# Steady pairs of the fast matrix product: P2 beside P7 instead of P5, and T4 made by VectorE from P2's tile

## The chip, the cores and the metric

The kernel runs on one core of a Trainium2 chip. The core has a matrix engine (TensorE), three engines for elementwise work (VectorE, ScalarE, GpSimd), an engine that mostly issues transfers (SyncE), and 16 DMA engines between the chip's memory and the on-chip buffers. The metric is the device time of one execution in microseconds (us), the median of several runs. In views of the profile PE is TensorE's matmuls, PEld its weight loads, DVE VectorE, ACT ScalarE, POOL GpSimd and SP SyncE.

## The reference, cut to what matters

Two layers of a mixer with 512 tokens of width 2048 in f32. Each layer normalises, multiplies by a wide input matrix w_in, runs an attention, a short convolution and a cross-attention on parts of the result, gates them and multiplies by an output matrix w_o.

```python
for l in range(DEPTH):
    h = rmsnorm(x, pre_norm_g[l])
    z = h @ w_in[l]
    q_lat, kv_lat, k_pe, gb, gc, xin, q_mem, gate = split_cols(z)
    ...
    y = jnp.concatenate([a_out, c_out, m_out], axis=-1) * jax.nn.silu(gate)
    o = y @ w_o[l]
    x = x + rmsnorm(o, post_norm_g[l])
```

The change touches only how part of `h @ w_in[l]` is computed.

## The kernel before

**The product.** `z = h @ w_in` is done in column groups. A group takes two column blocks of w_in, 512 wide each (416 in the group of the latents), and multiplies them by h with seven half-size products instead of eight (the scheme of Strassen and Winograd). h is cut into four quarters A11, A12, A21, A22 by tokens and by depth, the group's weights into B11, B12 (upper half of the depth, first and second column block), B21, B22 (lower half). The left operands (A11, A12, A22 and four sums S1 to S4) are made once a layer (`combine`, L394) and kept. The right operands are, with the signs as the code has them: P1 uses B11, P2 uses B21, P5 uses T1 = B11 + B12, P6 uses T2 = T1 + B22, P4 uses T4 = T2 + B21, P3 uses B22, P7 uses B22 + B12. T1, T2 and T4 grow in place, in the tile "T" that was loaded as B11.

**Blocks.** Each product runs over its depth in four blocks, c = 0 to 3. One block is a unit of weights (128 partitions x 1024 values, or 832) and 12 matmuls: two token tiles, two depth tiles, three matmuls each (`mm3`, L250). Three, because every f32 operand is split in a high part in the engine's f32r format and a low part, and high by high, high by low and low by high are added up. So the second matmul of a block needs the low part of the weights, the first only the high part. A product's result stays in PSUM until c = 3; `ended` (L463) then evacuates it with ScalarE or VectorE into the output tiles.

**Preparing a unit.** `prep` (L158) issues, for each unit, a cast on ScalarE (L177, tile "wh") and a subtraction on VectorE (L178, tile "wl") of the raw weights "wr". The pools of high and low parts have three buffers each; so the cast of a block waits until TensorE is done with the block three before it. Sums listed in a unit's `sums` are added before the split (L168), those in `then` after it (L186). If a later product uses the same tile with more added, `more` (L152) issues an accumulating DMA from GpSimd's queue (L137) right after the split.

**Loading.** `load` (L140) issues a unit's DMA on SyncE's queue (also L137), in the order of the units, up to eight units beyond the step at hand. Raw tiles "wr" live in a pool of eight buffers (`RAW, PIECES, SLABS = 8, 4, 19`); a load waits, on SyncE, until a buffer is free, which is when the last operation on the tile that held it has ended. The loads behind it in SyncE's queue wait too.

**Order.** TensorE, SyncE and GpSimd run in the program's order throughout. ScalarE and VectorE do so only in the opening stage; after it their order is a planner's, made when the program is built. A layer has five groups of w_in: two with the order HEAD, then three with the order STEADY: "gm, qm" (gate part and memory queries), "lat" (the latents, 416 columns) and "ga" (gate parts). The output projection uses SECOND and LATE. In an order such as `[["P1"], ["P5", "P2"], ...]` an inner list is a pass over c, in which the named products take turns. In the last steady group of a layer two small steps of four transposes each (`turn4`, L764) follow every second block, from the group's 17th block to its 28th and last.

**Buffers in a steady group.** T holds four raw buffers from P1 to P4. P2's four tiles are loaded into the other four, and each is freed after its split; B22's four tiles follow into these (P3, and after accumulating B12, P7). The next group's T comes into the buffers that P7's splits free, its P2 tiles into those that P4's splits free.

**Lazy work.** Elementwise work that is not urgent is put on a list; each step has a `room` (L551) that says how much of it may be issued beside it.

Of the kernel before, what the change touches and what calls it, by code (L numbers as in the profile page):

```python
# [207 lines left out]
def encoder(tc, x, mem, positions, pre_norm_g, w_in, q_norm_g, w_uq, kv_norm_g, w_ukv, conv_w,  # L208
# [200 lines left out]
        split("S3", a21)  # L409

    HEAD = [["P1"], ["P2"], ["P5"], ["P6", "P3"], ["P7"], ["P4"]]
    STEADY = [["P1"], ["P5", "P2"], ["P6", "P3"], ["P7"], ["P4"]]
    SECOND = [["P2"], ["P1"], ["P5"], ["P6", "P3"], ["P7"], ["P4"]]
    LATE = [["P2"], ["P1"], ["P5", "P6", "P3"], ["P7"], ["P4"]]

    def group(left, key, w, block, slot, passes, final, hold=None, by_two=False, direct=None):
# [24 lines left out]
        def unit(q, c):  # L441
            def of(name, loads=(), more=None, sums=(), then=(), **kw):
                at = {"B11": (0, 0), "B12": (0, 1), "B21": (1, 0), "B22": (1, 1)}
                k = lambda n: (key, n, c)
                return Unit(k(name), {k(to): [block(*at[n], c)] for to, n in loads}, more and block(*at[more], c),
                            [(k(a), k(b)) for a, b in sums], [(k(a), k(b)) for a, b in then], **kw)
            if q == "P1":
                return of("P1" if apart else "T", [("P1" if apart else "T", "B11")])
            if q == "P2":
                return of("P2", [("P2", "B21")])  # L450
            if q == "P4":
                return of("T", more="B21", alloc=hold)
            if late:
                return {"P5": lambda: of("T", [("B12", "B12")], sums=[("T", "B12")], place=place),
                        "P6": lambda: of("T", [("B22", "B22")], sums=[("T", "B22")]),
                        "P3": lambda: of("B22", then=[("B12", "B22")]),
                        "P7": lambda: of("B12")}[q]()
            return {"P5": lambda: of("T", [("T", "B11")] if apart else [], more="B12"), "P6": lambda: of("T", more="B22"),
                    "P3": lambda: of("B22", [("B22", "B22")]), "P7": lambda: of("B22", more="B12")}[q]()
# [3 lines left out]
        def ended(q, tt):  # L463
            ps = bk[q][tt][:, :w]
            s = {(i, j): slot(i, j, tt) for i in range(2) for j in range(2)}
            if q == "P1":
                if apart:
                    nc.scalar.copy(s[1, 0], ps)
                elif passes is STEADY:
                    nc.scalar.copy(s[0, 0], ps)  # L470
# [79 lines left out]

        def room(q, c):  # L551
            if c < 3:
                return 0.2 if late and q in ("P5", "P6", "P3") else 1.4
            moves = {"P1": shared, "P2": not shared, "P5": apart, "P7": 1 + apart, "P4": apart or direct is not None}
            return (0.2 if late and q in ("P5", "P6", "P3") else 1.4) - 1.4 * moves.get(q, 1)

        out = []
        for k, names in enumerate(passes):
            if names == ["P4"] and hold:
                out.append([(whole("P4"), [unit("P4", c) for c in range(4)], 4.0)])  # L560
                continue
            steps = [(step(q, c), [unit(q, c)], room(q, c)) for c in range(4) for q in names]
            if names == ["P7"] and hold:
                steps[1:] = [s + (4,) for s in steps[1:]]
            if by_two and k == 0:
                steps[:2] = [(two(names[0], 0), [unit(names[0], c) for c in range(2)], 0.0, 1)]
            out.append(steps)
# [58 lines left out]
    def projection(l):  # L626
        def block(cols, w):
            def f(h, j, c):
                r = h * 1024 + c * 256
                return w_in[l, r:r + 256, cols[j]:cols[j] + w].rearrange("(a p) c -> p a c", p=P)  # L630
            return f
# [9 lines left out]
        def slot_of(a, b):  # L641
            return lambda i, j, tt: C[(a, b)[j]][:, 2 * i + tt, :]
# [17 lines left out]
        def own_lat():  # L660
# [8 lines left out]
            group(L, (l, 1), 512, block((O_GB, O_G + 1024), 512), slot_of("gb", "gg"), HEAD, fin_g),  # L669
            group(L, (l, 2), 512, block((O_G + 1536, O_QM), 512), slot_of("gm", "qm"), STEADY, skip),  # L670
            group(L, (l, 3), 416, block((0, 416), 416), lat, STEADY, skip),
            group(L, (l, 4), 512, block((O_G, O_G + 512), 512), slot_of("ga0", "ga1"), STEADY, skip),
        ]
# [102 lines left out]
    def gate_turn(j, view, c):  # L776
        def f():
            ps = turn4(view, c)
            nc.scalar.activation(y_slab(j // 4)[:, j % 4, :], ps, AF.Silu)
        return f  # L780
# [13 lines left out]
    def qm_turn(j, C):  # L794
        def f():
            if j == 0:
                G["Qm"] = tuple(slab(n, F32R).rearrange("p (i c) -> p i c", i=4) for n in ("QmH", "QmL"))
            ps = turn4(lambda t: C["qm"][:, t, :], j)
            hi, lo = G["Qm"][0][:, j, :], G["Qm"][1][:, j, :]
            nc.scalar.activation(hi, ps, AF.Copy, scale=SC_MEM)  # L800
            nc.vector.scalar_tensor_tensor(lo, ps, SC_MEM, hi.bitcast(F32), op0=ALU.mult, op1=ALU.subtract)
        return f
# [480 lines left out]
    for l in range(depth):  # L1283
# [83 lines left out]
        more = [(f, []) for f in lat + [qm_turn(j, C) for j in range(4)] + [gate_turn(12 + j, gm, j) for j in range(4)]]  # L1367
# [76 lines left out]
```

## Time and profile before

| | us |
|---|---|
| median of 3 runs (lowest, highest) | 1505.4 (1505.35, 1508.21) |
| the profiled execution | 1509.11 |
| its span, first to last instruction | 1507.3 |
| granted TensorE clock, mean | 0.998 |
| transfers | 267.19 MB, mean 177 GB/s |
| accumulating and other transfers of GpSimd's queue | 45.0% of 16 engines' span |
| transfers of SyncE's queue | 27.9% |

How to read it: the page is one execution on the chip. Busy time is the time in which an engine has an instruction of its own; matmul ends are modelled, so for TensorE the distance between the starts of matmuls says more than busy time. In a row of the groups by line stand line, engine, operation, output<-inputs, form and count, then busy us and mean ns, then the engine's idle time ahead of these instructions and who ended it. In the timeline a row is start, duration, engine, line, operation; what stands in square brackets is the idle time ahead and who ended it. The steady groups begin at about 174.5, 254.3 and 318.8 us in layer 0 and at 965.0, 1044.9 and 1108.0 us in layer 1.

### The profile page before, as it was taken

How to read it: one execution, taken by the hardware profiler on the slowest of the kernel's cores; microseconds unless marked ns; L12 is line 12 of the kernel's file. 1: busy time of each engine (PE TensorE's matmuls, PEld its weight loads, DVE VectorE, ACT ScalarE, POOL GpSimd, SP SyncE). 2: the span in 40 equal slices, each digit the busy share in tenths (PEclk: the TensorE clock that was granted, in tenths of full speed). 3: DMA queues.
4: the chain of work that ended last, by engine and by line, in shares of the span. 5: the costliest groups of instructions: out<-in, count | busy, mean ns of one | idle time of the engine just before them, and what ended most of it. 6: DMA issues, size and time to landing. Idle time of an engine off the chain costs nothing.

```text
span 1507.3 us, 20232 instructions
## 1 busy us (share of the span) xinstructions
PE 1487.8 (99%) x7613; PEld 1279.3 (85%) x7613; DVE 1055.9 (70%) x1420; ACT 871.5 (58%) x1359; POOL 285.0 (19%) x277
## 2 busy tenths in 40 slices
PE   9999999999999999999999999999999999999997
PEld 7788888988898888888898888788988888988886
DVE  6965675555877668769788765575565586698687
ACT  7743534454757868645688533534464587686443
POOL 1233131332000000130310233131333000003211
PEclk9999999999999999999999999999999999999999
DMA  9999897989582112595987999898999521028945
GB/s 331 217 214 224 200 177 168 190 209 250 164 259 84 62 30 69 99 213 163 314 300 233 236 222 214 203 174 168 198 211 211 157 71 43 29 84 140 253 123 182
DMA packets 142581, 267.19 MB, mean 177 GB/s; under 512 B 17084, under 2 KB 39956, under 8 KB 139156
## 3 DMA queue, kind: packets, MB, share of 16 engines
q0 software_dynamic: 59072, 128.99, 45.0%
q1 hardware_dynamic: 83280, 136.88, 27.9%
q8 instruction: 59, 0.97, 0.3%
q14 instruction: 38, 0.31, 0.1%
q10 hardware_dynamic: 132, 0.05, 0.0%
HBM read 251.20 MB, written 14.68 MB: 176 GB/s over the span
## 4 chain that ended last, share of the span: by engine, by line
PE 83%; issue 5%; ACT 3%; DMA 3%; POOL 3%; DVE 2%; POOLq 0%; DVEq 0%; ACTq 0%
PE P L253 19%; PE P L254 19%; PE P L252 19%; POOL wr L137 3%; PE ptp L1017 2%; DMA wr<-in_w_in_dram 2%; PE tps L768 2%; DMA wr<-in_w_o_dram 1%; PE o L253 1%; PE o L254 1%; PE o L252 1%; PE sc L252 1%; PE sc L253 1%; PE sc L254 1%; PE mk L253 1%
## 5 line engine op out<-in xcount | busy, mean ns | idle before, releaser
L178 DVE TENSOR_TENSOR wl<-wr,wh 128x1024 fp32r<-128x1024 f32 (+1 forms) x400 | 476.0, 1194 | 312.7 <-ACT wh L177 304.2
L177 ACT CAST wh<-wr 128x1024 fp32r<-128x1024 f32 (+1 forms) x400 | 411.4, 1032 | 456.6 <-PE P L254 372.4
L253 PE MATMUL P<-wl,S 128*128 128x512 f32 (+1 forms) x896 | 344.1, 384 | 2.2 <-DVE wl L178 2.0
L252 PE MATMUL P<-wh,S 128*128 128x512 f32 (+1 forms) x896 | 345.4, 386 | 0.3 <-ACT wh L177 0.3
L254 PE MATMUL P<-wh,S 128*128 128x512 f32 (+1 forms) x896 | 343.4, 383 | 0.0
L137 POOL DMA_DIRECT2D wr<-in_w_in_dram x160 | 193.5, 1209 | 483.3 <-DVE wl L178 353.6
L252 PE MATMUL P<-wh,A 128*128 128x512 f32 (+1 forms) x656 | 253.1, 386 | 0.1
L253 PE MATMUL P<-wl,A 128*128 128x512 f32 (+1 forms) x656 | 252.0, 384 | 0.8 <-DVE wl L178 0.8
L254 PE MATMUL P<-wh,A 128*128 128x512 f32 (+1 forms) x656 | 251.8, 384 | 0.5 <-DVE A L258 0.5
L253 PEld LDWEIGHTS P<-wl,S 128*128 128x128 f32 x896 | 168.2, 188 | 33.2 <-DVE wl L178 3.6
L252 PEld LDWEIGHTS P<-wh,S 128*128 128x128 f32 x896 | 168.1, 188 | 30.7 <-ACT wh L177 1.1
L254 PEld LDWEIGHTS P<-wh,S 128*128 128x128 f32 x896 | 168.2, 188 | 30.3
L137 POOL DMA_DIRECT2D wr<-in_w_o_dram x40 | 48.4, 1210 | 530.7 <-DVE wl L178 516.3
L254 PEld LDWEIGHTS P<-wh,A 128*128 128x128 f32 x656 | 123.1, 188 | 23.3 <-DVE A L258 1.2
L253 PEld LDWEIGHTS P<-wl,A 128*128 128x128 f32 x656 | 123.2, 188 | 23.0 <-DVE wl L178 1.6
L252 PEld LDWEIGHTS P<-wh,A 128*128 128x128 f32 x656 | 123.1, 188 | 22.2 <-ACT wh L177 0.6
L1003 ACT ACTIVATE P<-sc,nm 128x512 f32<-128x512 f32 (+1 forms) x96 | 59.7, 622 | 31.2 <-DVE nm L1000 31.2
L1006 ACT ACTIVATE P<-P,rec 128x512 f32<-128x512 f32 (+1 forms) x96 | 63.1, 660 | 6.6 <-DVE rec L1005 6.6
L1000 DVE TENSOR_REDUCE nm<-sc 128x1 f32<-128x512 f32 (+1 forms) x96 | 57.0, 593 | 9.7 <-PE sc L998 6.2
L258 DVE TENSOR_TENSOR PT<-ptp,PT 128x512 fp32r<-128x512 f32 (+1 forms) x96 | 54.8, 593 | 10.0 <-ACT PT L257 9.6
L183 DVE SCALAR_TENSOR_TENSOR wl<-wr,cols,wh 128x512 fp32r<-128x512 f32 x64 | 45.8, 746 | 13.5 <-ACT wh L182 13.5
L182 ACT ACTIVATE wh<-wr,cols 128x512 fp32r<-128x512 f32 x64 | 43.8, 723 | 19.0 <-PE mk L253 7.8
(281 smaller groups left out, 2208.4 us busy)
## 6 DMA issues: line engine op xcount, KB each, us to landing
wr<-in_w_in_dram POOLq DMA_DIRECT2D x128, 512.0 KB, 7.3
wr<-in_w_in_dram SPq DMA_DIRECT2D x112, 512.0 KB, 5.9
wr<-in_w_o_dram SPq DMA_DIRECT2D x48, 512.0 KB, 4.2
wr<-in_w_o_dram POOLq DMA_DIRECT2D x40, 512.0 KB, 7.3
wr<-in_w_in_dram POOLq DMA_DIRECT2D x32, 416.0 KB, 5.7
wr<-in_w_in_dram SPq DMA_DIRECT2D x24, 416.0 KB, 4.1
wr<-in_w_mk_dram SPq DMA_DIRECT2D x16, 512.0 KB, 6.1
wr<-in_w_mv_dram SPq DMA_DIRECT2D x16, 512.0 KB, 5.4
```

What stands on the lines that cost most here:

```text
L137: engine.dma_start(dst, src, **kw)
L177: nc.scalar.copy(hi[:, :n], src)
L178: nc.vector.tensor_tensor(lo[:, :n], src, hi[:, :n].bitcast(F32), op=ALU.subtract)
L182: nc.scalar.activation(hi[:, h], src[:, h], AF.Copy, scale=g)
L183: nc.vector.scalar_tensor_tensor(lo[:, h], src[:, h], g, hi[:, h].bitcast(F32), op0=ALU.mult, op1=ALU.subtract)
L252: nc.tensor.matmul(ps, ah, bh, start=first, stop=False, **kw)
L253: nc.tensor.matmul(ps, ah, bl, start=False, stop=False, **kw)
L254: nc.tensor.matmul(ps, al, bh, start=False, stop=last, **kw)
L258: nc.vector.tensor_tensor(lo, src, hi.bitcast(F32), op=ALU.subtract)
L1000: nc.vector.tensor_reduce(nmax, ps, axis=AX.X, op=ALU.max, negate=True)
L1003: nc.scalar.activation(pt, ps, AF.Exp, bias=nmax, accum_out=tot)
L1006: nc.scalar.activation(pt, pt, AF.Copy, scale=rec)
```

## The change

In the order STEADY, P2 leaves the pass of P5 and takes turns with P7. After the split of P2's unit c, VectorE adds P2's tile (B21) into T (which holds T2 by then), and the accumulating DMA that added B21 to T for P4 goes away. P2's steps leave less room for lazy work. HEAD, SECOND and LATE stay as they are.

```diff
-    STEADY = [["P1"], ["P5", "P2"], ["P6", "P3"], ["P7"], ["P4"]]
+    STEADY = [["P1"], ["P5"], ["P6", "P3"], ["P7", "P2"], ["P4"]]
...
             if q == "P2":
-                return of("P2", [("P2", "B21")])
+                return of("P2", [("P2", "B21")], then=[("T", "P2")] if passes is STEADY else ())
             if q == "P4":
-                return of("T", more="B21", alloc=hold)
+                return of("T", more=None if passes is STEADY else "B21", alloc=hold)
...
         def room(q, c):
             if c < 3:
+                if passes is STEADY and q == "P2":
+                    return 0.4
                 return 0.2 if late and q in ("P5", "P6", "P3") else 1.4
```

## The prediction

> **What bounds the kernel now.** I read the page's busy times first, then TensorE's waits, then the stretches of the three steady groups in each layer, then the order of events inside one group.
>
> ```profile
> PE 1487.8 (99%) x7613; PEld 1279.3 (85%) x7613; DVE 1055.9 (70%) x1420; ACT 871.5 (58%) x1359; POOL 285.0 (19%) x277
> ```
> ```profile
> 254.30:318.80 64.50, 63.64 (x337) 62.49 (x336) 32.70 (x37) 31.96 (x49) 18.72 (x16) 1.00 0.95 202
> ...
> sum 450.50, PE 449.64 PEld 393.42 DVE 271.87 ACT 214.79 POOL 124.29; mean PE 74.94 PEld 65.57 DVE 45.31 ACT 35.80 POOL 20.71
> ```
>
> The first column pair is the stretch and its length, then busy time by engine, granted clock, DMA share, GB/s. TensorE is the bound: over the six steady groups (450.50 us) it sits idle 0.86 us, all of it in the latents group of layer 0, where the DMA engines are 95% busy. So the change can only win back what stands in this place:
>
> ```profile
> 305.92 0.34 PE L254 MATMUL P<-wh,S 128*128 128x416 f32 x1
> 306.52 0.46 PE L252 MATMUL P<-wh,S 128*128 128x416 f32 x1 [0.26 <-ACT wh L177]
> 307.58 0.46 PE L253 MATMUL P<-wl,S 128*128 128x416 f32 x1 [0.60 <-DVE wl L178]
> 307.88 0.35 PE L254 MATMUL P<-wh,S 128*128 128x416 f32 x1
> 308.07 0.35 PE L252 MATMUL P<-wh,S 128*128 128x416 f32 x1
> ```
> ```profile
> 295.98 9.51 DMA wr<-in_w_in_dram
> 305.48 0.02 issue
> 305.50 0.04 ACTq L177
> 305.54 0.04 issue
> 305.58 0.90 ACT wh L177
> ```
> ```profile
> 305.58 2.46 ACT L177 CAST wh<-wr 128x832 fp32r<-128x832 f32 x3 [5.15 <-DMA wr<-in_w_in_dram]
> ```
>
> Matmuls of 416 columns start 0.19 us apart. Here the starts are 0.60, 1.06 and 0.30 apart, so the stall costs 0.41 + 0.87 + 0.11 = 1.4 us. It is P7 with c = 3: its accumulating DMA took 9.51 us to land, between the accumulates of P4. The last row shows what a late transfer does on ACT: after 5.15 us of idleness it ran three casts back to back, so the two behind the waiting one had stood in its queue. ACT starts 0.1 us after the landing (295.98 + 9.51 = 305.49, cast at 305.58).
>
> What decides the forecast is another resource, the eight raw buffers. In a steady group four hold T from P1 to P4 and the other four hold P2's tiles, then B22's. SyncE's loads wait for them:
>
> ```profile
> SPq L137 <- DVE wl L178: 28.7, 8, 12.9
> ```
> ```profile
> 228.36 1.22 DVE L178 TENSOR_TENSOR wl<-wr,wh 128x1024 fp32r<-128x1024 f32 x1 [1.49 <-ACT wh L177]
> ```
> ```profile
> 229.61 0.37 SPq L137 DMA_DIRECT2D wr<-in_w_in_dram  x1
> ```
> ```profile
> 229.61 4.70 DMA wr<-in_w_in_dram
> ```
> ```profile
> 232.51 0.39 PE L252 MATMUL P<-wh,S 128*128 128x512 f32 x1
> ...
> 235.23 0.39 PE L252 MATMUL P<-wh,S 128*128 128x512 f32 x1
> 235.46 0.39 PE L253 MATMUL P<-wl,S 128*128 128x512 f32 x1
> ```
>
> The first row is SyncE's own waits from 229 to 250 us (total, times, longest): all eight loads of that stretch, from P7 to the end of P4, were held back by a subtraction that had not yet freed its buffer. The next rows follow the first of them, from VectorE, SyncE, the chain of waits and TensorE in turn. The subtraction of P7's first block ends at 229.58, SyncE issues 0.03 us later, and that load lands after 4.70 us. P7's first block starts on TensorE at 232.51, the next at 235.23: a block takes 2.72 us, and its second matmul (0.23 us in) is the first that needs the low part. Before, that load was for the next group, many blocks ahead, so its wait cost nothing.
>
> **The change, part by part.** Prices of single operations:
>
> ```profile
> L178 DVE TENSOR_TENSOR wl<-wr,wh 128x1024 fp32r<-128x1024 f32 x344 | 418.8, 1222 | 252.3 <-ACT wh L177 243.8 <-PE ptp L1017 7.5
> L177 ACT CAST wh<-wr 128x1024 fp32r<-128x1024 f32 x344 | 361.8, 1055 | 393.2 <-PE P L254 316.0 <-DVE wr L168 27.5 <-DMA wr<-in_w_in_dram 17.7
> L137 POOL DMA_DIRECT2D wr<-in_w_in_dram x160 | 193.5, 1209 | 483.3 <-DVE wl L178 353.6 <-DMA wr<-in_w_in_dram 87.1 <-issue 19.3
> L178 DVE TENSOR_TENSOR wl<-wr,wh 128x832 fp32r<-128x832 f32 x56 | 57.2, 1025 | 60.5 <-ACT wh L177 60.4
> L177 ACT CAST wh<-wr 128x832 fp32r<-128x832 f32 x56 | 49.6, 889 | 63.5 <-PE P L254 56.4 <-DMA wr<-in_w_in_dram 7.1
> L168 DVE TENSOR_TENSOR wr<-wr,wr 128x1024 f32<-128x1024 f32 x8 | 9.8, 1221 | 0.1
> ```
>
> *Removed:* 24 of the 160 accumulates (4 x 3 groups x 2 layers), 24 x 1.21 = 29.0 us of GpSimd and 16 x 0.52 + 8 x 0.43 = 11.8 MB. GpSimd bounds nothing. The worth on the path is at most the 1.4 us stall; I take it whole, since P7's accumulates now come every second block with no P4 accumulates among them. Bounds: nothing, if another transfer is late there, and 1.4. **-1.4.**
>
> *Added:* 24 additions on VectorE, 16 x 1.22 + 8 x 1.02 = 27.7 us. VectorE is busy 271.87 of 450.50 us here, so the time fits. Queued behind each addition is the subtraction of P7's next block: it ends 2.44 us after P2's, and is wanted 2.72 us after. That margin of 0.28 covers it; without it the price is at most some 1 us a group, 6 in all, kept for the upper end. I take 0.
>
> *Moved with no price taken:* P2's two evacuations a group go beside P7's, both off the path. P6's accumulate now follows P5's preparation by four blocks instead of eight, 10.9 us less 2.7 for cast, subtraction and issue, against this landing time:
>
> ```profile
> wr<-in_w_in_dram POOLq DMA_DIRECT2D x128, 512.0 KB, 7.3
> ```
>
> The 0.9 us that remain cover it; a landing of 9.51 would cost 1.3 a group. SyncE's queue: P2's loads move behind B22's, and the next group's T and (layer 0, last group) mem's loads behind P2's, all wanted eight or more blocks later.
>
> *Moved, and on the path: P2's loads.* When P7's first block is prepared, T and B22 fill all eight buffers. P2's first tile can only be loaded after that subtraction, one block before TensorE wants it.
>
> First load, 512 columns, on the clock of the rows above (load at 229.61): landed 234.31, cast from 234.40 to 235.46, subtraction to 236.71, wanted 235.46: late by **1.3 us**.
>
> Second load: it takes whichever buffer is freed first, by the T4 addition at 236.71 + 1.22 = 237.93 or, if the casts keep program order, by P7's second subtraction after it. A quiet load:
>
> ```profile
> wr<-in_w_mv_dram SPq DMA_DIRECT2D x4, 512.0 KB, 3.8
> ```
> ```profile
> wr<-in_w_in_dram SPq DMA_DIRECT2D x7, 416.0 KB, 3.5
> ```
>
> Issued 237.96, landed 241.76, cast and subtraction 2.4: 244.16. Wanted two blocks after the first, 236.71 + 5.44 = 242.15: late by **2.0**. Each pair frees two buffers and uses one, so the third and fourth loads are issued about two blocks earlier than needed: 0.
>
> The 416-column group:
>
> ```profile
> 295.95 1.03 DVE L178 TENSOR_TENSOR wl<-wr,wh 128x832 fp32r<-128x832 f32 x1 [1.23 <-ACT wh L177]
> ```
> ```profile
> 299.34 0.35 PE L252 MATMUL P<-wh,S 128*128 128x416 f32 x1
> ...
> 301.59 0.35 PE L252 MATMUL P<-wh,S 128*128 128x416 f32 x1
> 301.78 0.35 PE L253 MATMUL P<-wl,S 128*128 128x416 f32 x1
> ```
>
> Load at 297.00 (after 296.98), landing +4.70 = 301.70, cast to 302.68, subtraction to 303.73, wanted 301.78: **1.95**. Second: 1.02 + 0.03 + 3.5 + 0.09 + 0.89 + 0.03 + 1.02 = 6.58, less two blocks of 2.25: **2.1**. In the last steady group two turns of four transposes follow each pair, 8 x 0.109 = 0.87 us of other TensorE work:
>
> ```profile
> 1189.27 3.93 PE tps L768 x36
> ```
>
> So there 1.3 and 2.0 - 0.87 = 1.1.
>
> *The waits this adds.* On ACT the cast of P2's tile waits for the landing; behind it in the queue is the cast of P7's next block, whose data is long there and whose subtraction would free the next buffer: hence the second load's lateness. On VectorE P2's subtraction waits for the cast, the T4 addition and P7's next subtraction for it. On SyncE P2's load waits for the buffer, and behind it stand the next three and the next group's T. TensorE waits for P2's low part, and since it is the bound each of its waits is added to the end; it works off the blocks behind at 2.72 us each and makes nothing up.
>
> The unknown is the landing time: 4.70 is the row with the same neighbours (an accumulate issued just ahead), 3.3 the quickest, 9.51 the slowest. I take 4.70 for the first, the quiet medians for the second.
>
> ```profile
> wr<-in_w_in_dram SPq DMA_DIRECT2D x1, 416.0 KB, 3.3
> ```
>
> The Trainium skill, DMA: Bandwidth & Descriptors, section "Anatomy of one DMA", gives a DMA as 2.0 us and its bytes over 436 GB/s; my estimate from it is 3.2 us for 512 KB and 3.0 for 416, and the sum would then be +5.2. The trace has 3.8 and 3.5 when quiet, 4.70 beside an accumulate, so the rows decide.
>
> **Sum.** A layer: (1.3 + 2.0) + (1.95 + 2.1) + (1.3 + 1.1) = 9.75; two layers 19.5; less 1.4: **+18.1 us**. The profiled execution is 1507.3 of span and 1.8 around it, 1509.1, so it would be 1527.2. The median shown is 1505.4, 3.7 below it; I forecast on the median: 1523.5, own range 1517 to 1530.
>
> **The rivals.**
>
> *Casts out of program order.* ACT's order is the planner's there. Does it put P7's second cast before P2's first, that buffer is freed before 236 and the second load is in time. Then the first loads alone remain: 2 x (1.3 + 1.95 + 1.3) = 9.1, less 1.4: +7.7, 1513. For it: ACT would have idled. Against: the three casts in a row at 305.58.
>
> *Quick loads.* Each lands in 3.3 us, as in the row above. First loads 0, 0.55, 0; second 1.4, 1.9, 0.5: 4.35 a layer, 8.7 - 1.4 = +7.3, 1513. This is the side on which the Trainium skill's formula for a DMA lies. Against: the accumulate for P7's last block is in flight at the first load.
>
> *No slower.* Both together at the first and second P2 block: only 2 x 0.55 remains against the 1.4 won, -0.3, 1505. It decides where the load after P7's first subtraction lands within 3.4 us and P7's second cast goes ahead. More than 1.4 us cannot come from these groups, so faster by over 3 us has no mechanism I can find.
>
> *Late in every pair.* If the second buffer of a pair isn't freed before the next load wants it, three loads a group pay the second price: (1.3 + 6.0) + (1.95 + 6.3) + (1.3 + 3.3) = 20.15 a layer, +38.9, 1544. Against: two buffers are freed a pair.
>
> **How the numbers follow.** Forecast 0.50, order 0.20, quick loads 0.10, no slower 0.12, late in every pair 0.05, faster 0.03. A measurement tells some 0.2%, 3 us, from no change. Slower: 0.50 + 0.20 + 0.10 + 0.05 = 0.85; same 0.12; faster 0.03. The range takes in the forecast's own and both cases at 1513, and ends in the middle of the "no slower" case: 1506 to 1532.
>
> **What would show it.** In each steady group TensorE waits on ACT's cast and then VectorE's subtraction at P2's first and second block, 1 to 2 us each, released by a DMA of SyncE, whose issue follows the first subtraction of P7 by 0.03 us. The waits of SyncE name that subtraction and L186's addition. The wait at 306 is gone. Wrong if P2's tiles are loaded before P7 begins, or if P2's blocks show no wait on TensorE.

## The result, and the profile after

The changed kernel takes 1524.5 us in the median of 4 runs (1523.3 to 1526.5), the kernel before 1506.1 (1505.4 to 1508.2). The ratio is 1.0119, 95% interval 1.0107 to 1.0132: slower by 18 us. The profiled execution of the changed kernel is the fastest of its four, 1523.3 us with a span of 1521.4, while that of before, 1509.1 us with a span of 1507.3, was slower than its four; so the two traces lie only 14.1 us apart. The forecast was 1523.5.

The page after, and TensorE's waits (what waited, for whom; total us, times, longest):

```profile
PE 1492.3 (98%) x7613; PEld 1280.2 (84%) x7613; DVE 1082.1 (71%) x1444; ACT 870.5 (57%) x1359; POOL 256.1 (17%) x253
```
```profile
PE P L253 <- DVE wl L178: 6.9, 11, 0.8
PE P L252 <- ACT wh L177: 6.1, 7, 2.6
```

VectorE has 24 instructions and 26 us more, GpSimd 24 fewer and 29 us less, as reckoned. TensorE has the same 7613 matmuls. What grew is its waits for a cast (0.3 us before) and for a subtraction (2.8 before), in the three steady groups of each layer. The worst of the six stretches, before and after, and the six together after (length, busy time by engine, clock, DMA share, GB/s):

```profile
1044.90:1108.00 63.10, 63.10 (x338) 62.58 (x337) 33.74 (x46) 32.22 (x49) 19.03 (x16) 1.00 0.98 207
```
```profile
1052.20:1120.70 68.50, 65.33 (x337) 63.96 (x337) 38.37 (x53) 31.87 (x49) 14.31 (x12) 0.98 0.75 166
...
sum 466.20, PE 454.54 PEld 393.62 DVE 297.84 ACT 213.08 POOL 95.35; mean PE 75.76 PEld 65.60 DVE 49.64 ACT 35.51 POOL 15.89
```

TensorE sits idle 11.7 us here instead of 0.9, and the DMA engines are less busy than before (0.75 in the latents group of layer 1, 0.98 before). So the kernel waits in a stage with fewer transfers, not more: it waits for the start of one. The chain of waits in the first steady group (start, length, what):

```profile
217.25 1.24 DVE wl L178
218.49 0.02 issue
218.50 5.24 DMA wr<-in_w_in_dram
223.74 0.02 issue
223.76 1.22 DVE wr L186
224.99 1.17 DVE wl L178
226.15 0.02 issue
226.17 3.97 DMA wr<-in_w_in_dram
230.14 0.02 issue
230.16 1.23 DVE wr L186
231.39 1.18 DVE wl L178
232.57 0.04 issue
232.61 0.50 PE P L253
```

This is the forecast chain but for one step, the second load. P7's first subtraction ends at 218.48, and the load of P2's first tile is issued at 218.50; the subtraction of that tile ends at 226.15, and the load of the second tile goes at 226.17, where the forecast had it wait for the addition behind that subtraction. All six second loads leave 0.02 us after the subtraction of P2's first tile. TensorE between them, and ACT's casts:

```profile
223.90 0.39 PE L254 MATMUL P<-wh,S 128*128 128x512 f32 x1
224.94 0.49 PE L252 MATMUL P<-wh,A 128*128 128x512 f32 x1 [0.65 <-ACT wh L177]
226.20 0.50 PE L253 MATMUL P<-wl,A 128*128 128x512 f32 x1 [0.76 <-DVE wl L178]
```
```profile
223.84 1.99 ACT L177 CAST wh<-wr 128x1024 fp32r<-128x1024 f32 x2 [6.62 <-DMA wr<-in_w_in_dram]
230.24 2.95 ACT L177 CAST wh<-wr 128x1024 fp32r<-128x1024 f32 x3 [4.40 <-DMA wr<-in_w_in_dram]
```

The tile names show the place: P7 reads S, P2 reads A. The first P2 matmul starts 1.04 us after its predecessor and the second 1.26 us after that, where 0.227 is the pace. ACT sat idle for 6.62 us and then ran P2's cast and, right behind it, the one of P7's next block.

The time lost at P2's blocks, summed from the starts of TensorE's matmuls as far as they are over 0.227 us apart (0.189 in the latents groups), in us; the forecast's pairs are the first and the second block:

| group (layer, name) | first P2 block | second | forecast |
|---|---|---|---|
| 0, gm and qm | 1.95 | 0.95 | 1.3, 2.0 |
| 0, latents | 2.33 | 0.81 | 1.95, 2.1 |
| 0, ga | 1.98 | 0 | 1.3, 1.1 |
| 1, gm and qm | 1.86 | 0.51 | 1.3, 2.0 |
| 1, latents | 4.48, and 0.63 at the next block | 0 | 1.95, 2.1 |
| 1, ga | 1.60 | 0 | 1.3, 1.1 |
| sum | 14.2 + 0.6 | 2.3 | 9.1, 10.4 |

Together 17.1 us, against 19.5 forecast; the third and fourth P2 blocks lose nothing. Less the 1.4 us of P7 in the latents group of layer 0, which are gone, and 2.0 at three other last blocks of P7 outside the steady groups, which are shorter in this trace (0.96, 1.38 and 0.40 us became 0.69, 0 and 0), that is 13.7 of the 14.1 us between the spans.

### The profile page after: what moved, and what is told of

Same layout as the page of the kernel before. It is cut to its first block, busy times and chain, and to the rows that moved or that the text cites. A ratio compares the mean times of both kernels' runs of the same rounds, so it can differ in the third digit from the quotient of the medians.

```text
span 1521.4 us, 20175 instructions
## 1 busy us (share of the span) xinstructions
PE 1492.3 (98%) x7613; PEld 1280.2 (84%) x7613; DVE 1082.1 (71%) x1444; ACT 870.5 (57%) x1359; POOL 256.1 (17%) x253
## 4 chain that ended last, share of the span: by engine, by line
PE 88%; DMA 3%; DVE 3%; ACT 3%; issue 1%; POOL 1%; POOLq 0%; DVEq 0%; ACTq 0%
PE P L253 20%; PE P L254 20%; PE P L252 20%; DMA wr<-in_w_in_dram 3%; PE ptp L1019 2%; PE tps L770 2%; DVE wl L178 1%; PE o L253 1%; PE o L254 1%; PE o L252 1%; PE sc L252 1%; PE sc L253 1%; PE sc L254 1%; PE mk L253 1%; PE mk L254 1%
## 5 line engine op out<-in xcount | busy, mean ns | idle before, releaser
L137 POOL DMA_DIRECT2D wr<-in_w_in_dram x136 | 164.6, 1211 | 499.3 <-DVE wl L178 376.4
L182 ACT ACTIVATE wh<-wr,cols 128x512 fp32r<-128x512 f32 x64 | 43.8, 723 | 19.5 <-PE mk L253 7.9
```

Of the source, the lines that this page charges most:

```text
L137: engine.dma_start(dst, src, **kw)
L182: nc.scalar.activation(hi[:, h], src[:, h], AF.Copy, scale=g)
```

## The experiments

The theory is the one of the forecast: eight raw buffers, all held when P7 begins, so that P2's loads start one block before they are wanted (their lead is one block). The rivals put the time down to the 24 additions on VectorE, to slow transfers, or to P2's evacuations beside P7's. The ratios are against the kernel before.

### A pass of its own for P2

```diff
-    STEADY = [["P1"], ["P5"], ["P6", "P3"], ["P7", "P2"], ["P4"]]
+    STEADY = [["P1"], ["P5"], ["P6", "P3"], ["P7"], ["P2"], ["P4"]]
```

> P2 gets a pass of its own between P7 and P4, so its tiles are loaded as P7's subtractions free the buffers, four blocks before they are wanted; T4 is still made by VectorE. Buffer theory: no wait of TensorE at any P2 block, the 18 us come back whole, 1503 to 1507 us (ratio to the kernel before 0.998 to 1.000). Rival, the additions on VectorE or the later evacuations cost the time: 1515 or more, with waits at P2 or P4.

Measured: 1507.3 us (before, on the same chip, 1506.7), ratio 1.0005, interval 0.9995 to 1.0015. The time is at the upper end of the expected range, a little above it. All additions are there and all the accumulates are gone; P2 comes later, and the lead of its loads is longer. No P2 block waits; TensorE's waits for a cast and a subtraction are back to what they were:

```profile
PE P L253 <- DVE wl L178: 2.2, 3, 0.8
...
PE P L252 <- ACT wh L177: 0.4, 2, 0.2
```

So the additions cost nothing that can be measured. P2's evacuations no longer stand beside P7's here; the next run has them there. One part of the expectation failed: the 1.4 us of P7's stall don't come back. In this trace P7 of the same group still loses 0.95 us, one block earlier.

### One more block of lead

```diff
             steps = [(step(q, c), [unit(q, c)], room(q, c)) for c in range(4) for q in names]
+            if names == ["P7", "P2"]:
+                steps = [steps[n] for n in (0, 2, 1, 4, 3, 6, 5, 7)]
```

> The changed kernel with the pass of P7 and P2 shifted by one block: P7, P7, P2, P7, P2, P7, P2, P2. Every P2 load has two blocks of lead instead of one. Buffer theory: the lead of the first load grows by 2.72 us (2.25 in the latents group) and that of the second too, so the waits go in the 512-column groups and at most 1.5 us is left in each latents group: 1505 to 1511. Rival, P2 beside P7 costs by its additions or evacuations: 1520 or more.

Measured: 1506.9 us, ratio 1.0004, interval 0.9995 to 1.0013, with no wait at any block of the six groups, not even in the latents groups, where up to 1.5 us had been allowed for. TensorE's waits for a subtraction are these two, at 48.6 and 678.2 us, outside the groups:

```profile
PE P L253 <- DVE wl L178: 1.3, 2, 0.8
```

P2 still takes turns with P7, and the additions and the smaller room for lazy work are those of the changed kernel. So the whole loss goes with the lead. A lead of two blocks is enough; one is not.

### The order alone

```diff
-                return of("P2", [("P2", "B21")], then=[("T", "P2")] if passes is STEADY else ())
+                return of("P2", [("P2", "B21")])
...
-                return of("T", more=None if passes is STEADY else "B21", alloc=hold)
+                return of("T", more="B21", alloc=hold)
```

> The new order alone: P2 beside P7, but T4 by the accumulating DMA as before, no addition on VectorE. Buffer theory: the same waits at the first two P2 blocks of a group, the first load landing up to 2 us later because P4's accumulates are in flight again: 1524 to 1534. Rival, the additions are what costs: 1505 to 1510.

Measured: 1534.6 us, ratio 1.0190, interval 1.0169 to 1.0211. The loss is there without a single addition, and larger, because P4's accumulates are in the way of the first load. The chain in the latents group of layer 0:

```profile
289.94 8.52 DMA wr<-in_w_in_dram
...
298.56 0.89 ACT wh L177
...
299.48 1.04 DVE wl L178
```

The load took 8.52 us to land, with three accumulates still in flight when it was issued, and 7.6 us are lost at this block (6.9, 6.1 and 6.8 in three of the other groups; 1.8 and 1.9 in gm and qm, where two were in flight and the first loads took 5.1 and 5.2 us). Of each of the four large losses 1.6 to 2.0 us are the lower clock of the last section. The profiled execution (1541.1 us) is the slowest of the four. So the two halves of the change belong together: the additions take the accumulates out of the way of the load that the order has made urgent.

### P2's tiles in slabs

```diff
-                return of("P2", [("P2", "B21")], then=[("T", "P2")] if passes is STEADY else ())
+                return of("P2", [("P2", "B21")], then=[("T", "P2")] if passes is STEADY else (),
+                          **({"place": place} if passes is STEADY and key[1] != 3 else {}))
```

> The changed kernel, with P2's tiles of the first and the last steady group of each layer in two of the large slabs instead of raw buffers; the latents group stays. Buffer theory: the waits at P2 go in these four groups (1.85 + 0.84, 1.87, 1.75 + 0.40 and 1.50 us in the trace of the changed kernel, 8.2 in all) and stay in the latents groups: 1514 to 1518. Rival, P2 beside P7 is late whatever its buffer: 1522 to 1527.

Measured: 1517.6 us, ratio 1.0057, interval 1.0037 to 1.0078. At the P2 blocks of the four groups nothing is lost any more; in the two latents groups 3.8 and 3.2 us are. The order and the additions are the changed kernel's, only the buffers differ, and with them the time of the loads. (The 8.2 us of the expectation are 8.9 in the table above, which also counts the third matmul of a block.)

In the profiled execution (1521.2 us, the slowest of the four) two other blocks lose time. P7's last block ahead of layer 1's first steady group loses 4.7 us, after an accumulate of 10.38 us; in the kernel before, the same accumulate took 9.52 us and 1.38 us were lost. P2's early loads are not the cause, since the first of them in that layer is issued at 974.14 us; why the accumulate took longer stays open. In the steady group itself P7's first block loses 1.3 us: ScalarE's planned order there casts P2's first tile, now in a slab ("B"), ahead of P7's.

```profile
943.95 10.38 DMA wr<-in_w_in_dram
```
```profile
1016.63 1.06 ACT L177 CAST wh<-B 128x1024 fp32r<-128x1024 f32 x1 [1.67 <-PE P L254]
1019.35 1.04 ACT L177 CAST wh<-wr 128x1024 fp32r<-128x1024 f32 x1 [1.66 <-PE P L254]
```

### The addition behind the subtraction

```diff
-                return of("P2", [("P2", "B21")], then=[("T", "P2")] if passes is STEADY else ())
+                return of("P2", [("P2", "B21")], then=[("P2", "T")] if passes is STEADY else ())
...
-                return of("T", more=None if passes is STEADY else "B21", alloc=hold)
+                return of("P2") if passes is STEADY else of("T", more="B21", alloc=hold)
```

> The changed kernel, but the sum goes into P2's tile (P2 = P2 + T) and P4 reads it there. The addition now writes what P2's subtraction reads, so it must stand behind it, and the buffer that it frees is T's: the sequence that the prediction had reckoned with. If the second load's smaller price came from the addition running beside the cast, the second load now leaves 1.2 us later and its waits grow to 2.0, 2.1 and 1.1 us in the three groups of a layer, 7 to 9 us in all over the changed kernel: 1529 to 1535. If the second load was early for another reason: 1522 to 1527.

Measured: 1527.1 us, ratio 1.0137, interval 1.0123 to 1.0151. The chain in the first steady group:

```profile
224.66 0.04 DVE wl L178
224.70 1.11 issue
225.80 1.23 DVE wl L178
227.05 3.64 DMA wr<-in_w_in_dram
```

The planner put P7's second subtraction (225.80) next, and the second load leaves after it, 1.16 us after P2's own subtraction instead of 0.02 us. The second blocks lose 1.75, 1.78, 0.78, 1.75, 1.80 and 0.74 us: 8.6 in all against 2.3 in the changed kernel, and near the forecast's 2.0, 2.1 and 1.1. The total is only 2.5 us above the changed kernel's and lies between the two expected ranges, so it alone doesn't decide; the second blocks in the trace do. The rise is smaller than theirs because the first blocks lost 11.6 us in this trace against 14.8, the latents group of layer 1 being 2.2 instead of 4.48 + 0.63.

### One buffer a pair, tried in vain

```diff
-                return of("P2", [("P2", "B21")], then=[("T", "P2")] if passes is STEADY else ())
+                return of("P2", [("P2", "B21")])
...
-                return of("T", more=None if passes is STEADY else "B21", alloc=hold)
+                return of("T", more=None if passes is STEADY else "B21", alloc=hold,
+                          sums=[("T", "P2")] if passes is STEADY else ())
```

> The changed kernel, but P2's tile is added to T ahead of P4's split instead of behind P2's own, so each P2 tile keeps its buffer until P4 and a pair of blocks frees one buffer, not two. Buffer theory: all four P2 loads of a group are late, the first as now (1.5 to 2.2 us), the next three by some 1.7 (0.9 in the last steady group): 37 us in all over the kernel before, 1538 to 1548. Rival, the loads are late because the transfers are slow: no change from the changed kernel, 1522 to 1527.

Measured: 1522.2 us, ratio 1.0099, interval 1.0086 to 1.0113, near the changed kernel and far from the 37 us expected. The premise didn't hold. VectorE's order in the first steady group:

```profile
223.35 1.23 DVE L168 TENSOR_TENSOR wr<-wr,wr 128x1024 f32<-128x1024 f32 x1 [1.55 <-DMA wr<-in_w_in_dram]
224.50 2.36 DVE L178 TENSOR_TENSOR wl<-wr,wh 128x1024 fp32r<-128x1024 f32 x2
```

L168 is the addition that the code issues ahead of P4's split. It ran when P2's tile had landed, before even P2's own subtraction: the planner takes what its data allow, so no buffer was held. The run tells nothing for or against either theory, and what a pair that frees one buffer costs stays untried.

### What the accumulates are worth

```diff
-                return of("T", more="B21", alloc=hold)
+                return of("T", more=None if passes is STEADY else "B21", alloc=hold)
```

> The kernel before with P4's accumulate of B21 left out in the steady groups and nothing in its place, so P4 there lacks one of its four parts. It shows what the removal of 24 accumulates can win by itself. Theory: at most the one stall of 1.4 us at P7 in the latents group of layer 0: 1504 to 1507 (ratio 0.998 to 1.000). Rival, the accumulates slow the path elsewhere too: 1502 or less.

Made on the kernel before. Measured: 1506.1 us, ratio 0.9995, interval 0.9986 to 1.0004. The stall of 1.4 us at P7 is gone from its trace (0.7 us are lost at a P2 block of the ga group in layer 0 instead), but in the time of the whole nothing is won that can be measured.

## Why the prediction was right, and where not

*Bound and bottleneck:* right. TensorE's waits carry the loss, and each of those in the steady groups is at a P2 block, after a load that SyncE issued 0.02 us after a subtraction had freed its buffer. Other buffers (slabs, in the four groups that have them), a pass of its own or one more block of lead each takes these waits away. Two of the signs that the forecast named came out otherwise: the second blocks wait 0.5 to 1.0 us in three groups and not at all in the other three, and SyncE's waits ahead of the second loads name P2's subtraction, not the addition.

*The removed accumulates, -1.4:* too high. Without them the stall at 306 goes, yet a kernel with nothing else changed gains 0.05%, within its interval; in its trace 0.7 us are lost at another block of the same layer. The stall was read in an execution of 1509.1 us and taken off a median of 1505.4; whether executions near the median have it isn't shown. The lower bound, nothing, was the right value. What the removal does is protect the first load: the order alone costs 10 us more than the change.

*The additions, 0:* right for the time, wrong for the place. The reckoning had each addition behind P2's subtraction, ending 1.22 us after it. The trace has it ahead: 223.76 on VectorE, beside the cast at 223.84: it needs only the landed tile and T, and the planner put it first. So it is over when the subtraction begins, at 224.99.

*First load, 1.3, 1.95, 1.3 a layer:* right as a mechanism, too small. It rested on a landing of 4.70 us, and that row is a load of 416 KB, a tile of the latents group that came next; P2's tiles in the 512-column groups are 512 KB. There the first loads took 4.88 to 5.24 us, as far as the trace has their landings, and 6.27 us in the latents group of layer 1. The size of the load behind the 4.70, from the kernel before, and the worst landing:

```profile
wr<-in_w_in_dram SPq DMA_DIRECT2D x1, 416.0 KB
```
```profile
1085.98 6.27 DMA wr<-in_w_in_dram
```

Sum 14.2 + 0.6 us instead of 9.1. Of the 5.1 in the latents group of layer 1, part isn't the load's own (below).

*Second load, 2.0, 2.1, 1.1:* right as a mechanism, too large: 2.3 us in all instead of 10.4. The step that failed is "freed first by the T4 addition at 236.71 + 1.22": the buffer was freed by P2's own subtraction, 1.2 us earlier. When the addition is made to stand behind it, the second blocks lose 8.6 us, so this step is most of the error; five of the six second loads also landed sooner than the rows used.

*Third and fourth loads, 0:* right.

So the sum came out by two errors that nearly cancel, 5.7 too little and 8.1 too much in the profiled execution. The mechanism was the forecast one, but that the median was hit within 1 us is luck: its terms were not that exact.

*The rivals:* casts stayed in program order (two, then three in a row on ACT); the first loads were slower, not quicker, than the row used, while the second ones took 3.13 to 3.97 us against 3.5 and 3.8; two buffers came free a pair. The Trainium skill's formula in DMA: Bandwidth & Descriptors, section "Anatomy of one DMA" (2.0 us and the bytes over 436 GB/s, my estimate 3.2 us for 512 KB and 3.0 for 416), is given there for transfers that GpSimd issues, and these loads are SyncE's. Here a 512 KB load with no accumulate in flight took 3.97 us and one right behind an accumulate 5.24; a 416 KB load among P4's accumulates took 8.52, which its bytes don't explain.

## What to carry to other kernels

Here a load's place in its queue didn't set when it started; the buffer that it went into did. Before moving a product or a stage, count at each step which buffers are held and which operation frees the next one, and compare the lead from that operation to the use with the landing time under the load of that stage; here one block (2.72 us) decided over 18 us. And where a price hangs on the order of two operations on one engine, ask what each of them needs: where a planner sets the order, as here, the one whose data are there first can go first, against the order of the source.

## What was not expected of the hardware

The granted clock fell after some of the late loads, so that TensorE lost more than its wait. In the latents group of layer 1 of the changed kernel it idled 2.56 us, ran one matmul, idled 0.61, ran four matmuls at the usual pace, and then its starts were 0.35 us apart instead of 0.19:

```profile
1093.29 0.45 PE L252 MATMUL P<-wh,A 128*128 128x416 f32 x1 [2.56 <-ACT wh L177]
1094.35 0.46 PE L253 MATMUL P<-wl,A 128*128 128x416 f32 x1 [0.61 <-DVE wl L178]
...
1095.46 0.55 PE L252 MATMUL P<-wh,A 128*128 128x416 f32 x1
1095.81 0.55 PE L253 MATMUL P<-wl,A 128*128 128x416 f32 x1
```

Some ten matmuls lost 0.16 us each this way, 1.5 us on top of the 3.7 that the wait had cost.

The length of the wait alone doesn't decide it: with P2's tiles in slabs idle times of 1.57 and 0.61 us, with a single matmul between them, were enough, and at another place 1.02 and 0.61 were; in the changed kernel 1.20 and 0.60 us were not. What does separate them in these nine traces is a fixed grid. The half clock always begins a whole number of spans of 3.41 us after the full clock began (319 of them in the changed kernel), and ahead of the end of the program it lasts one such span, or two in the kernel with the order alone. Two neighbouring spans of the grid in three kernels: changed, with slabs, and with the addition behind the subtraction (the clock is the third number from the end):

```profile
1091.90:1095.31 3.41, 1.41 (x6) 1.14 (x7) 2.96 (x3) 1.67 (x2) 0.00 (x0) 1.00 0.00 0
1095.31:1098.72 3.41, 3.41 (x12) 3.23 (x11) 1.25 (x2) 1.17 (x2) 0.00 (x0) 0.50 0.79 250
```
```profile
1091.04:1094.45 3.41, 1.78 (x9) 1.16 (x8) 2.81 (x3) 1.67 (x2) 0.00 (x0) 1.00 0.01 2
1094.45:1097.86 3.41, 3.41 (x12) 3.24 (x11) 0.96 (x2) 0.74 (x1) 0.00 (x0) 0.50 0.80 247
```
```profile
296.26:299.67 3.41, 2.02 (x9) 1.74 (x10) 2.65 (x3) 1.52 (x2) 0.00 (x0) 1.00 0.00 0
299.67:303.08 3.41, 3.06 (x17) 2.68 (x15) 0.25 (x1) 0.65 (x1) 0.00 (x0) 1.00 0.78 246
```

TensorE is idle for 2.00, 1.63 and 1.39 us in the first span of each pair. Over all nine traces it is idle for at least 1.63 us in the span ahead of every fall, and for at most 1.61 in every span after which the full clock stayed. So the same wait can cost the clock or not, by where it lies on the grid. That this limit holds for other kernels isn't shown. The Trainium skill, TensorE: Matmul & The Clock Gate, Part 1, has the clock fall to half after an idle window of some 3.4 us; the length agrees with the 3.41 us here, but TensorE was busy for up to 1.78 us of the span ahead of a fall.
